# Moving output copies into two-buffer slots, pooling stores to another queue, and the last stage's loads a chunk ahead

## The chip, the core and the metric

The kernel runs on one NeuronCore of a Trainium2 chip. The metric is the device time of one execution in microseconds (us); lower is better. TensorE (PE) does the matrix products, VectorE (DVE), ScalarE (ACT) and GpSimd (POOL) the elementwise work, and SyncE (SP) and ACT issue the DMAs, each from a queue of its own.

## The reference, cut to what matters

One layer of a hybrid encoder: a normed input goes through one projection, whose columns feed three groups. Sizes: 2048 rows, width 1024, 256 memory tokens, groups of width 512, 4 heads of 128.

```python
h = rmsnorm(x, norm_g)
proj = h @ w_in                                   # (2048, 1024) @ (1024, 5128)
qk_raw, v, o, z_a, gates, u, z_b, qc, z_c = split(proj)
y_a = mlstm(conv(qk_raw), v, o, gates) * silu(z_a)     # chunked recurrence, per head rmsnorm
y_b = pool(u) * silu(z_b)                              # window means of 2, 4, 8, 16, minus u, @ pool_w
km, vm = split(rmsnorm(mem, mem_norm_g) @ w_kv)        # 256 memory tokens
y_c = (softmax(qc @ km.T / sqrt(128)) @ vm) * silu(z_c)
x = x + concat([y_a, y_b, y_c]) @ w_out
return rmsnorm(x, final_norm_g)
```

All of it is float32.

## The kernel before, in words

Products are made in three TensorE passes of "fp32r" parts: a tensor is split into a high half (ACT copies it) and a low half (DVE or POOL subtracts), and `mm3` (L152, L155, L156) multiplies high by high, high by low and low by high.

The projection is tiled into **quads**: a block of 2x2 tiles, 2 blocks of 512 rows by two column halves, computed with seven products in place of eight (Winograd's form of Strassen). The quad's combined inputs are the forms `A11`, `A12`, `S1` to `S4`, `A22`, held as tiles `xA`, `xS` (split at L198 on ACT and L199 on DVE); combined weights are the tiles `wf`. Kinds of quad: `run_tok` (the columns v, o, z_a, rows as partitions; results go to the DRAM scratch `d_t`), and channel quads for the convolution, for pooling and for attention. The sequence of 2048 rows is done in two halves s=0 and s=1. Order: one `run_tok` quad with the memory tokens' products laid in between (the first stage), four pairs of convolution and pooling quads, four attention quads, two `run_tok` quads, and for s=1 two `run_tok` quads, four pairs, four attention quads, one `run_tok` quad. Then the output stage runs over 16 chunks of 128 rows.

Work is placed between the products by a list: `later(n, f)` puts `f` n ticks ahead, and each product ends with `tick()`. A scheduler then sets each engine's order from the program and a timeline; each engine runs its list strictly in that order, and a wait stops all behind it. Tiles come from pools: a tag has a number of buffers, and a new tile of a tag waits until the last use of the oldest one is over, its store to DRAM too.

What the change touches:

- `ev` (L141) gives the tiles in which PSUM is copied out. The tags `s1` and `u2` have two buffers each; all other names share the tag `e` with one buffer: `dg` of `bcast` (L163, four diagonals made from row factors at L166, from which the product at L168 broadcasts them to all partitions), `c11` (L420), `c12` (L435), `ga` and `q1`. `run_tok` has for each of its two blocks `bk` the results s1, c11, u2, c12 in turn, and `store` (L397) issues their DMA on ACT's queue (in the trace these tiles are `c`, `s`, `u`, and the DMA is `d_t<-c`).
- `first(n)` (L596) is the list of the first stage: `mem_k`, `mem_v` (keys and values of the memory tokens, 12 products of 128x512 for each `mem_v(q)`), `scale_y` (L183, eight rows `y`, which needs `dg`) and the forms of the next quad.
- `pooling`'s `end` (L844) multiplies by the gate into `zb` and stores its two halves at L847 on SP's queue.
- `load_y(c)` (L956) loads 128 rows of y_b and y_c as `yr` (L959, SP), copies the high half on ACT (`ybh`, L962) and the low half on POOL (`ybl`, L963). It is called for c = 0 during the last `run_tok` quad, for c = 1 ahead of the output stage, and for c + 2 inside chunk c's turn. All `yr` share one slot, `x0`.
- In the attention quads `th` (L782) copies the transposed probabilities for the product with the values.
- The output stage: `out_k(c, i)` (L982) adds twelve steps per chunk, the first eight from y_b and y_c, the last four from y_a. `cell(c)` (L1026) is the recurrence of chunk c: `Ab` gets the mask on POOL (L1029), `Dm` is its exponential on ACT (L1034), multiplied by the scores on DVE (L1048) and used by the products at L1062; the head norm goes `sq` (ACT, L1089), `ss` (DVE, L1090, then POOL's power, L1091), `hh` (DVE, L1093); the transpose of `hh` (L1098) is y_a.

Of the kernel before, what the change touches and what calls it, by code (L numbers as in the profile page):

```python
# [18 lines left out]
P = 128  # L19
# [7 lines left out]
GW = 512  # L27
# [25 lines left out]
def hybrid_block(tc, xT, xn, memT, wch, wuT, wtok, wgt, wkm, wvm, wo, pw, cols, bg, gf, out):  # L53
# [33 lines left out]
    with ExitStack() as outer:  # L87
# [73 lines left out]
            G.tensor_tensor(dst, ms[:, :w], mhalf[:, :w], ALU.pow)  # L161

        def bcast(src_cols, w):  # L163
            dg = ev("dg", shape=(P, 4, P))
            for i in range(w):
                V.tensor_scalar(dg[:, i], ident, src_cols[:, i:i + 1], None, ALU.mult)  # L166
            pb = bank([P, 4, P], "aux")
            tc.keep_in_program_order(T.matmul(pb[:, :w], ones, dg[:, :w], start=True, stop=True))  # L168
            return pb[:, :w].rearrange("p a b -> p (a b)")
# [220 lines left out]
        def run_tok(q, step=None, pinned=False):  # L390
# [9 lines left out]
            for n, (xfm, wfm, acc, opens) in enumerate(q.order):  # L400
# [5 lines left out]
                for bk in range(2):  # L406
                    pp = banks[acc][bk]
                    for r in range(2):
                        sl = slice((2 * bk + r) * P, (2 * bk + r + 1) * P)
                        for k in range(4):  # L410
                            wh, wl = q.forms[wfm][k]
                            xt = xf[xfm][k]
                            mm3(pp[:, r], xt[:, 0, sl], xt[:, 1, sl], wh, wl, opens and k == 0 and r == 0, k == 3,
                                pin=k == 0 and (opens and r == 1 or pinned and r == 0))
                    pf = pp.rearrange("p a b -> p (a b)")
                    if n == 0:
                        s1[bk] = ev("s1")
                        A.activation(s1[bk], pf, AF.Copy)
                    elif n == 1:
                        c11 = ev("c11")  # L420
                        A.activation(c11, pf, func)
                        store(c11, 0, 0, bk)
                    elif n == 2:
                        u2[bk] = ev("u2")
                        V.tensor_tensor(u2[bk], pf, s1[bk], ALU.add)
                    elif n == 3:
                        V.tensor_tensor(s1[bk], pf, u2[bk], ALU.add)
                    elif n == 4:
                        t = s1[bk]
                        V.tensor_tensor(t, pf, t, ALU.add)  # L430
                        if n_:
                            A.activation(t, t, func)
                        store(t, 1, 1, bk)
                    elif n == 5:
                        t = ev("c12")  # L435
                        V.tensor_tensor(t, pf, u2[bk], ALU.add)
                        if n_:
                            A.activation(t, t, func)
                        store(t, 0, 1, bk)
                    else:  # L440
                        t = u2[bk]
                        V.tensor_tensor(t, pf, t, ALU.add)
                        if n_:
                            A.activation(t, t, func)
                        store(t, 1, 0, bk)
                    if bk == 1:
                        used(q, wfm)
                    tick()
# [147 lines left out]
        def first(n):  # L596
# [9 lines left out]
            elif n == 2:  # L606
                scale_y(0, y, 1)
                xs["pre"]()
                Wv.append(mem_w(wvm[0], [P, 2, GW]))
            elif n == 3:  # L610
                mem_k(3, W[3])
                mem_k_out(3)
                Wv.append(mem_w(wvm[1], [P, 2, GW]))
                xs["S2"]()
            elif 4 <= n < 8:
                mem_v(n - 4, Wv[n - 4])
                if n < 6:
                    Wv.append(mem_w(wvm[n - 2], [P, 2, GW]))
            for m, f in ((5, "S1"), (6, "S3"), (8, "S4"), (10, "A22")):
                if n == m:  # L620
                    xs[f]()
        for n in range(12):
# [191 lines left out]
        def pooling(q):  # L814
# [10 lines left out]
            def sums():  # L825
# [18 lines left out]
                def end():  # L844
                    V.tensor_tensor(z, cur[0][:, HL:], z, ALU.mult)
                    for i in range(2):
                        dma(d_y[2 * s + i][:, :, g, :], z[:, i * BW:(i + 1) * BW].rearrange("p (a b) -> p a b", a=4))  # L847
                n = win.bit_length() - 1
                for i in range(n):
                    (add if i == 0 else lambda st: later(i, lambda: add(st)))(1 << i)  # L850
# [87 lines left out]
        def prep_wo(i):  # L938
# [12 lines left out]
            else:  # L951
                g = col[:, C_OG + k:C_OG + k + 1]
                A.activation(woh[k], raw, AF.Copy, scale=g)
                V.scalar_tensor_tensor(wl, raw, g, r32(woh[k]), ALU.mult, ALU.subtract)

        def load_y(c):  # L956
            b, cc = divmod(c, 4)
            yr = xp.tile([P, 8, P], F32, name="yr", tag="x0")
            dma(yr, d_y[b][:, cc])  # L959
            yh = xp.tile([P, 8, P], F32R, name="ybh", tag=f"x{1 + c % 2}")  # L960
            yl = (fp if c % 2 else xp).tile([P, 8, P], F32R, name="ybl", tag="ybl" if c % 2 else "x3")
            A.activation(yh, yr, AF.Copy)  # L962
            G.tensor_tensor(yl, yr, r32(yh), ALU.subtract)  # L963
            return yh, yl

        def last_step(n):
            if n == 2:
                ybs[0] = load_y(0)
            elif n > 2:
                prep_wo(2 * n - 6)  # L970
                prep_wo(2 * n - 5)
# [19 lines left out]
                T.matmul(outs[c][n], l, w[:, n * 512:(n + 1) * 512], start=i == 0 and p_ == 0, stop=i == KO - 1 and p_ == 2)  # L991


        ybs[1] = load_y(1)
        gfb = fp.tile([P, D], F32, name="gfb", tag="gfb")
        dma(gfb, gf.partition_broadcast(P))

# [154 lines left out]
        for c in range(NT):  # L1152
            xr = st([P, D], "xr")
            dma(xr, xn[c * P:(c + 1) * P])
            if c + 1 < NT:
                outs[c + 1] = [bank([P, 512], "mm") for n in range(2)]
                for i in range(8):
# [2 lines left out]
                    out_k(c + 1, i, ybs[c + 1])  # L1160
                    tick()
                    if i == 1 and c + 2 < NT:
                        ybs[c + 2] = load_y(c + 2)
                    if i == 5 and c + 2 < NT:
                        load_chunk(c + 2)
                while c not in yas or (c == NT - 2 and due):
# [60 lines left out]
```

## Time and profile before

| | before |
|---|---|
| device time, median of 3 runs | 1254.31 us (1253.19 to 1255.76) |
| the profiled execution, its own time | 1250.7 us |
| its span, first to last instruction | 1248.9 us |
| PE busy | 1178.2 us, 94% |
| DVE busy | 747.8 us, 60% |
| ACT busy | 481.4 us, 39% |
| POOL busy | 201.8 us, 16% |
| mean granted TensorE clock | 0.976 of full |

The profiled execution is 3.6 us under the median, and 1.8 us of it lie outside the span. The page's first part gives busy times, the second forty slices of the span with the granted clock, the fifth the groups of instructions with the idle time ahead of them. A bracket such as `[2.99 <-ACT th L782]` behind an instruction is the idle time of its engine before it, and what ended that idle time.

### The profile page before, as it was taken

How to read it: one execution, taken by the hardware profiler on the slowest of the kernel's cores; microseconds unless marked ns; L12 is line 12 of the kernel's file. 1: busy time of each engine (PE TensorE's matmuls, PEld its weight loads, DVE VectorE, ACT ScalarE, POOL GpSimd, SP SyncE). 2: the span in 40 equal slices, each digit the busy share in tenths (PEclk: the TensorE clock that was granted, in tenths of full speed). 3: DMA queues.
4: the chain of work that ended last, by engine and by line, in shares of the span. 5: the costliest groups of instructions: out<-in, count | busy, mean ns of one | idle time of the engine just before them, and what ended most of it. 6: DMA issues, size and time to landing. Idle time of an engine off the chain costs nothing. (4 is left out here: it accounts for less than half of the span.)

```text
span 1248.9 us, 17606 instructions
## 1 busy us (share of the span) xinstructions
PE 1178.2 (94%) x6579; PEld 1019.4 (82%) x6579; DVE 747.8 (60%) x1318; ACT 481.4 (39%) x947; POOL 201.8 (16%) x154
## 2 busy tenths in 40 slices
PE   6659999996999899999999999998989999999997
PEld 5649888885888899899778887887978888888886
DVE  5876478976677448842564554554536565656434
ACT  7434454433676434440421224554433222222211
POOL 1321121112001011300000000000035232324120
PEclk9879999999999999999999999998989999999999
DMA  9615877789455698437667775546595545454511
GB/s 355 215 42 203 308 278 281 264 290 317 179 180 191 210 363 301 164 120 246 208 197 227 256 245 207 161 152 219 150 321 163 190 146 179 149 179 145 169 51 68
DMA packets 123925, 258.75 MB, mean 207 GB/s; under 512 B 9792, under 2 KB 65856, under 8 KB 123328
## 3 DMA queue, kind: packets, MB, share of 16 engines
q1 hardware_dynamic: 91680, 230.36, 53.6%
q10 hardware_dynamic: 32160, 27.27, 6.7%
q8 instruction: 52, 0.85, 0.3%
q14 instruction: 33, 0.27, 0.1%
HBM read 158.96 MB, written 98.63 MB: 206 GB/s over the span
## 5 line engine op out<-in xcount | busy, mean ns | idle before, releaser
L307 ACT ACTIVATE wf<-wr 128x512 fp32r<-128x512 f32 x120 | 74.6, 628 | 116.0 <-PE mm L156 66.1
L308 DVE TENSOR_TENSOR wf<-wr,wf 128x512 fp32r<-128x512 f32 x120 | 85.0, 717 | 47.0 <-ACT wf L307 47.0
L152 PE MATMUL mm<-xS,wf 128*128 128x512 f32 x256 | 101.5, 396 | 1.8 <-DVE s L377 1.8
L156 PE MATMUL mm<-xS,wf 128*128 128x512 f32 x256 | 101.3, 396 | 0.0
L155 PE MATMUL mm<-xS,wf 128*128 128x512 f32 x256 | 100.9, 394 | 0.0
L991 PE MATMUL mm<-woh,ybh 128*128 128x512 f32 x256 | 94.8, 405 | 0.0
L991 PE MATMUL mm<-wol,ybh 128*128 128x512 f32 x256 | 92.6, 397 | 0.0
L991 PE MATMUL mm<-woh,ybl 128*128 128x512 f32 x256 | 89.9, 394 | 0.0
L152 PE MATMUL mm<-xA,wf 128*128 128x512 f32 x224 | 89.4, 401 | 0.0
L156 PE MATMUL mm<-xA,wf 128*128 128x512 f32 x224 | 88.5, 395 | 0.0
L155 PE MATMUL mm<-xA,wf 128*128 128x512 f32 x224 | 88.1, 393 | 0.0
L963 POOL TENSOR_TENSOR ybl<-yr,ybh 128x1024 fp32r<-128x1024 f32 x16 | 39.2, 2452 | 196.4 <-ACT ybh L962 156.7
L648 DVE SCALAR_TENSOR_TENSOR cacc<-text,col,cacc 128x1024 f32<-128x1024 f32 x48 | 65.4, 1373 | 8.1 <-ACT cacc L645 7.9
L1093 DVE SCALAR_TENSOR_TENSOR hh<-hh,ss,gz 128x128 f32<-128x128 f32 x64 | 51.4, 862 | 31.2 <-POOL ss L1091 31.2
L156 PE MATMUL pt<-wf,xS 128*128 128x256 f32 x192 | 56.8, 296 | 9.9 <-DVE xS L199 9.9
L152 PE MATMUL pt<-wf,xS 128*128 128x256 f32 x192 | 56.6, 295 | 7.5 <-ACT xS L198 6.2
L291 POOL TENSOR_TENSOR wr<-wr 128x512 f32<-128x512 f32 (+1 forms) x16 | 27.0, 1688 | 218.4 <-DVE wf L308 218.4
L156 PE MATMUL mm<-wf,xA 128*128 128x256 f32 x192 | 55.2, 287 | 4.1 <-DVE xA L199 4.1
L152 PEld LDWEIGHTS mm<-xS,wf 128*128 128x128 f32 x256 | 48.6, 190 | 11.8 <-DVE s L377 2.2
L156 PEld LDWEIGHTS mm<-xS,wf 128*128 128x128 f32 x256 | 48.4, 189 | 11.0
L991 PEld LDWEIGHTS mm<-woh,ybl 128*128 128x128 f32 x256 | 48.1, 188 | 10.7
L155 PEld LDWEIGHTS mm<-xS,wf 128*128 128x128 f32 x256 | 48.5, 190 | 9.9
(303 smaller groups left out, 3260.9 us busy)
## 6 DMA issues: line engine op xcount, KB each, us to landing
wr<-in_wch_dram SPq DMA_DIRECT2D x20, 512.0 KB, 5.4
y<-in_xT_dram SPq DMA_DIRECT2D x32, 256.0 KB, 6.4
wr<-in_wtok_dram SPq DMA_DIRECT2D x16, 512.0 KB, 5.9
d_qk<-cacc ACTq DMA_DIRECT2D x32, 256.0 KB, 4.8
yr<-d_y SPq DMA_DIRECT2D x16, 512.0 KB, 4.5
qk<-d_qk SPq DMA_DIRECT2D x16, 512.0 KB, 3.9
gz<-d_t SPq DMA_DIRECT2D x16, 512.0 KB, 3.7
xr<-in_xn_dram SPq DMA_DIRECT2D x16, 512.0 KB, 3.6
```

Source lines behind the costliest of these rows:

```text
L152: ins = T.matmul(po, ah, bh, start=first, stop=False, skip_group_check=True)
L155: T.matmul(po, ah, bl, start=False, stop=False, skip_group_check=True)
L156: T.matmul(po, al, bh, start=False, stop=last, skip_group_check=True)
L291: G.tensor_tensor(B["B11"], B["B12"], B["B11"], ALU.subtract)
L307: A.activation(t[:, 0], part, AF.Copy)
L308: V.tensor_tensor(t[:, 1], part, r32(t[:, 0]), ALU.subtract)
L648: V.scalar_tensor_tensor(c, t[:, i:i + 2 * BW], w(i), c, ALU.mult, ALU.add)
L963: G.tensor_tensor(yl, yr, r32(yh), ALU.subtract)
L991: T.matmul(outs[c][n], l, w[:, n * 512:(n + 1) * 512], start=i == 0 and p_ == 0, stop=i == KO - 1 and p_ == 2)
L1093: V.scalar_tensor_tensor(hh[:, h], hh[:, h], ss[:, h:h + 1], gz[:, 1, h], ALU.mult, ALU.mult)
```

## The change

Five things. The tiles `dg` and `c11` take the tag `u2`, and `c12` the tag `s1`, in place of the single buffer `e`. In `first`, each `mem_v` is run one step earlier, and the form `S4` too; `S2` is listed with the other forms, behind `mem_v(0)`. The two stores of each pooling quad go through `dma_out`, which is ACT's queue. `load_y` only issues the load, and `split_y` makes the two halves; the load for chunk c+3 follows the split for chunk c+2, and the raw rows alternate between the slot `x0` and a tile of the last stage's own pool. Loads 1 and 2 and the split of 1 stand ahead of the output stage.

```diff
-            dg = ev("dg", shape=(P, 4, P))
+            dg = ev("dg", shape=(P, 4, P), tag="u2")
...
-                        c11 = ev("c11")
+                        c11 = ev("c11", tag="u2")
...
-                        t = ev("c12")
+                        t = ev("c12", tag="s1")
...
-            elif n == 3:
-                mem_k(3, W[3])
-                mem_k_out(3)
-                Wv.append(mem_w(wvm[1], [P, 2, GW]))
-                xs["S2"]()
-            elif 4 <= n < 8:
-                mem_v(n - 4, Wv[n - 4])
-                if n < 6:
-                    Wv.append(mem_w(wvm[n - 2], [P, 2, GW]))
-            for m, f in ((5, "S1"), (6, "S3"), (8, "S4"), (10, "A22")):
+            elif 3 <= n < 7:
+                if n == 3:
+                    mem_k(3, W[3])
+                    mem_k_out(3)
+                    Wv.append(mem_w(wvm[1], [P, 2, GW]))
+                mem_v(n - 3, Wv[n - 3])
+                if n < 5:
+                    Wv.append(mem_w(wvm[n - 1], [P, 2, GW]))
+            for m, f in ((3, "S2"), (5, "S1"), (6, "S3"), (7, "S4"), (10, "A22")):
...
-                        dma(d_y[2 * s + i][:, :, g, :], z[:, i * BW:(i + 1) * BW].rearrange("p (a b) -> p a b", a=4))
+                        dma_out(d_y[2 * s + i][:, :, g, :], z[:, i * BW:(i + 1) * BW].rearrange("p (a b) -> p a b", a=4))
...
+        yraw = {}
+
         def load_y(c):
             b, cc = divmod(c, 4)
-            yr = xp.tile([P, 8, P], F32, name="yr", tag="x0")
-            dma(yr, d_y[b][:, cc])
+            yraw[c] = (fp if c % 2 else xp).tile([P, 8, P], F32, name="yr", tag="yr" if c % 2 else "x0")
+            dma(yraw[c], d_y[b][:, cc])
+
+        def split_y(c):
+            yr = yraw.pop(c)
             yh = xp.tile([P, 8, P], F32R, name="ybh", tag=f"x{1 + c % 2}")
             yl = (fp if c % 2 else xp).tile([P, 8, P], F32R, name="ybl", tag="ybl" if c % 2 else "x3")
             A.activation(yh, yr, AF.Copy)
             G.tensor_tensor(yl, yr, r32(yh), ALU.subtract)
-            return yh, yl
+            ybs[c] = yh, yl
...
-                ybs[0] = load_y(0)
+                load_y(0)
+                split_y(0)
...
-        ybs[1] = load_y(1)
+        load_y(1)
+        load_y(2)
+        split_y(1)
...
-                        ybs[c + 2] = load_y(c + 2)
+                        split_y(c + 2)
+                        if c + 3 < NT:
+                            load_y(c + 3)
```

Three places show what the scheduler makes of it. The lines of the code behind the change are some four to seven higher in number.

PE in the first stage, where the last product of `mem_k` (`mm<-mhl`) ends; `pt<-wf,xS` is the first product of the form S2 and `aux<-mwh,mhl` the first of `mem_v(0)`. Before:

```order
L155 MATMUL mm<-mhl_188,mwh 128x256
L156 MATMUL mm<-mhl_188,mwl 128x256
L152 MATMUL pt<-wf,xS_0_648 128x256
L155 MATMUL pt<-wf,xS_0_648 128x256
L156 MATMUL pt<-wf,xS_0_648 128x256
```

And after:

```order
L155 MATMUL mm<-mhl_188,mwh 128x256
L156 MATMUL mm<-mhl_188,mwl 128x256
L152 MATMUL aux<-mwh,mhl_143 128x512
L155 MATMUL aux<-mwl,mhl_143 128x512
L156 MATMUL aux<-mwh,mhl_143 128x512
```

The twelve products of `mem_v(0)` stand ahead of S2's; before, they stood behind the first 24 of S2.

ACT where the output stage begins; `ybh` are the high halves of chunks 1, 2 and 3, `Dm` those of cells 0 and 1, `sq` that of cell 0. Before:

```order
L438 ACTIVATE c_8052<-c_8052 128x512
L397 DMA d_t_90<-c_8052 128x2x256
L444 ACTIVATE u_7807<-u_7807 128x512
L953 ACTIVATE woh_8136<-woraw,col 128x1024
L397 DMA d_t_91<-u_7807 128x2x256
L444 ACTIVATE u_7845<-u_7845 128x512
L953 ACTIVATE woh_8142<-woraw,col 128x1024
L397 DMA d_t_91<-u_7845 128x2x256
L1034 ACT_TABLE_LOAD
L1034 ACTIVATE Dm<-Ab,tcols 128x128 x8
L962 ACTIVATE ybh<-yr 128x1024
L1089 ACTIVATE sq,ss<-hh 128x128 x4
```

And after:

```order
L444 ACTIVATE u_7807<-u_7807 128x512
L397 DMA d_t_91<-u_7807 128x2x256
L952 ACTIVATE woh_8136<-woraw,col 128x1024
L444 ACTIVATE u_7845<-u_7845 128x512
L952 ACTIVATE woh_8142<-woraw,col 128x1024
L397 DMA d_t_91<-u_7845 128x2x256
L966 ACTIVATE ybh<-yr 128x1024 x2
L1041 ACT_TABLE_LOAD
L1041 ACTIVATE Dm<-Ab,tcols 128x128 x8
L1096 ACTIVATE sq,ss<-hh 128x128 x4
```

The split of chunk 2 has moved from between `Dm` and `sq` to ahead of both, and that of chunk 1 from ahead of `c_8052` to beside it.

POOL at the same place, from the last memset on. Before:

```order
L1029 TENSOR_TENSOR Ab<-Ab,mask 128x512 x2
L1036 TENSOR_TENSOR Eb<-qk,Eb 128x512
L963 TENSOR_TENSOR ybl<-yr,ybh 128x1024
L1091 TENSOR_TENSOR ss<-ss,mhalf 128x4
L1029 TENSOR_TENSOR Ab<-Ab,mask 128x512
L963 TENSOR_TENSOR ybl<-yr,ybh 128x1024
```

And after:

```order
L967 TENSOR_TENSOR ybl<-yr,ybh 128x1024
L1036 TENSOR_TENSOR Ab<-Ab,mask 128x512
L967 TENSOR_TENSOR ybl<-yr,ybh 128x1024
L1036 TENSOR_TENSOR Ab<-Ab,mask 128x512
L1043 TENSOR_TENSOR Eb<-qk,Eb 128x512
L1098 TENSOR_TENSOR ss<-ss,mhalf 128x4
L967 TENSOR_TENSOR ybl<-yr,ybh 128x1024
```

The low half of chunk 2 stood directly ahead of the power of cell 0's norm, and now stands between the two masks.

## Rows read from the trace of the kernel before

**Rows 1.** The page, part 1: busy us, share of the span, instructions

```profile
PE 1178.2 (94%) x6579; PEld 1019.4 (82%) x6579; DVE 747.8 (60%) x1318; ACT 481.4 (39%) x947; POOL 201.8 (16%) x154
```

**Rows 2.** Waits of PE: engine, line, releaser: us in total, times, longest

```profile
PE aux L152 <- ACT th L782: 8.5, 2, 5.5
...
PE aux L168 <- DVE dg L166: 7.3, 1, 7.3
...
PE pt L1062 <- issue: 5.2, 1, 5.2
```

**Rows 3.** Windows: stretch, length, busy us of five engines, granted clock, DMA share, GB/s

```profile
66.40:83.50 17.10, 6.71 (x24) 5.54 (x25) 14.75 (x18) 4.40 (x8) 5.76 (x4) 0.50 0.22 74
...
424.80:428.30 3.50, 3.50 (x19) 3.50 (x18) 0.00 (x0) 0.00 (x0) 0.00 (x0) 0.51 0.46 177
480.80:520.20 39.40, 37.67 (x292) 34.89 (x292) 39.40 (x60) 18.61 (x33) 13.03 (x9) 1.00 0.57 195
867.85:872.00 4.15, 4.14 (x17) 3.70 (x18) 2.56 (x3) 1.48 (x2) 0.00 (x0) 0.50 0.65 218
931.85:936.85 5.00, 5.00 (x22) 4.68 (x23) 2.27 (x11) 1.27 (x2) 2.36 (x1) 0.50 0.80 260
```

**Rows 4.** Timeline, DVE, first stage: start us, us, operation

```profile
50.40 1.21 DVE L519 TENSOR_TENSOR mwl<-mwraw,mwh 128x1024 fp32r<-128x1024 f32 x1
...
51.87 0.86 DVE L166 TENSOR_SCALAR dg<-ident,rt 128x128 f32<-128x128 f32 x4
```

**Rows 5.** Timeline, PE: the first two products of the first value product

```profile
83.53 0.40 PE L152 MATMUL aux<-mwh,mhl 128*128 128x512 f32 x1
83.77 0.39 PE L155 MATMUL aux<-mwl,mhl 128*128 128x512 f32 x1
```

**Rows 6.** Timeline, ACT, at the end of the two attention stages

```profile
421.90 0.60 ACT L421 ACTIVATE c<-mm 128x512 f32<-128x512 f32 x1 [2.06 <-DMA d_t<-c]
...
866.16 0.60 ACT L421 ACTIVATE c<-mm 128x512 f32<-128x512 f32 x1 [3.85 <-DMA d_t<-c]
```

**Rows 7.** Timeline, PE, at the same two places

```profile
423.03 0.49 PE L152 MATMUL aux<-th,vmhl 128*128 128x512 f32 x1 [2.99 <-ACT th L782]
...
867.86 0.79 PE L152 MATMUL aux<-th,vmhl 128*128 128x512 f32 x1 [5.50 <-ACT th L782]
```

**Rows 8.** The tile c: its stores, from issue to landing

```profile
DMA to landing us min/median/max: 2.1/3.9/9.1
```

**Rows 9.** The pooling stores: duration of the issue in ns, first and last

```profile
L847 SPq DMA_DIRECT2D d_y<-zb x16: 524/580/894, 193.0 to 746.6; - x16
```

**Rows 10.** Waits of SP's queue at these stores

```profile
SPq L847 <- DVE zb L845: 7.5, 6, 2.5
```

**Rows 11.** Waits of ACT at the weight copies

```profile
ACT wf L307 <- PE mm L156: 68.3, 34, 9.5
```

**Rows 12.** Timeline, ACT, start of the output stage: the split of chunk 2

```profile
924.28 1.06 ACT L962 ACTIVATE ybh<-yr 128x1024 fp32r<-128x1024 f32 x1 [4.19 <-DMA yr<-d_y]
```

**Rows 13.** Timeline, POOL, same place

```profile
925.47 2.35 POOL L963 TENSOR_TENSOR ybl<-yr,ybh 128x1024 fp32r<-128x1024 f32 x1 [5.47 <-ACT ybh L962]
927.92 1.03 POOL L1091 TENSOR_TENSOR ss<-ss,mhalf 128x4 f32<-128x4 f32 x1
```

**Rows 14.** Timeline, DVE, same place and the end of the last quad

```profile
896.51 1.28 DVE L954 SCALAR_TENSOR_TENSOR wol<-woraw,col,woh 128x1024 fp32r<-128x1024 f32 x1 [1.74 <-ACT woh L953]
...
900.09 3.37 DVE L954 SCALAR_TENSOR_TENSOR wol<-woraw,col,woh 128x1024 fp32r<-128x1024 f32 x1
...
931.07 0.68 DVE L1048 TENSOR_TENSOR Dm<-aux,Dm 128x512 f32<-128x512 f32 x1
```

**Rows 15.** Timeline, PE: the first product of chunk 1, and the gap

```profile
910.51 0.39 PE L991 MATMUL mm<-woh,ybh 128*128 128x512 f32 x1
...
931.86 0.77 PE L1062 MATMUL pt<-vt,Dm 128*128 128x129 f32 x2 [5.15 <-issue]
```

**Rows 16.** The tile yr: its loads, from issue to landing

```profile
DMA to landing us min/median/max: 3.8/4.5/9.0
```

## The prediction

> **What bounds the kernel now.** First the busy times: PE works 94% of the span [rows 1], so what does not shorten PE's own work can win only the remaining 6% and what is lost to a lower clock. Second, therefore, the list of what PE waits for [rows 2]; the reader should look there for waits whose releaser the change touches. Three stand out: 8.5 us on `th`, 7.3 us on `dg`, 5.2 us without a named releaser ahead of the product of `vt` and `Dm`. Third, windows around these places, for the granted clock: after each long gap PE runs for some microseconds at 0.50 to 0.51, which is 1.2 in place of 2.4 GHz [rows 3], so a gap costs more than its own length. Fourth, the timelines of the engine that PE waited for, to see what that engine itself stood at [rows 4, 6, 12 to 14]. The sum below is made against the profiled execution, 1250.7 us; the median of the runs is 3.6 us higher, and I add that at the end. About 0.2%, 2.5 us here, is what a measurement of this kernel can tell from no change.
>
> **The copies c11 and c12.** At the end of each attention stage ACT stands at the second c11: 2.06 us at 421.90 and 3.85 us at 866.16, released by the store of the first one, which holds the only buffer [rows 6]. Right behind it on ACT are the copies `th`, and PE has nothing else: its gaps are 2.99 and 5.50 us [rows 7]. ACT's order there is the same after the change, but c11 takes its second buffer of `u2`, so the first place gains 2.0 us and the second 3.85. What is left of the gaps is about 1.0 and 1.65 us, for the copies and the handover. The clock: PE then worked 3.50 us at 0.51 and 4.15 us at 0.50 [rows 3]; half of that is lost, 1.7 and 2.1 us. That so short a rest leaves the clock up is my choice, with a little taken off the first: 1.5 and 2.05. Together 3.5 and 5.9 us; if the clock falls all the same, 2.0 and 3.85.
>
> What it costs: `u2` now carries `dg`, two c11 and two u2 in turn. The first u2 of a `run_tok` quad takes the first c11's buffer and waits for its store. A product group of a block is 24 passes of 256 columns, 2.8 us at 0.118 us (half of the 0.24 us that a pass of 512 takes [rows 5]), so the use comes two groups, 5.6 us, behind c11. The store lands in 3.9 us as a median, 9.1 at most [rows 8]: usually nothing, at worst 3.5 us of DVE, in front of a PE that has other banks. I take 0 in five quads. In the quad of the second half's start, 457 to 520, the new order puts `dg` and the scaling of `y` ahead of the eviction of u2, and DVE is busy for all of 480.80 to 520.20 [rows 3] while PE works 37.67 of those 39.40 us. So PE can lose up to 2 us at the moved eviction, or gain up to the 1.7 us idle there, and some of the work that DVE starts earlier; 0, from -2 to +4.
>
> **The value products.** From 66.40 to 83.50 PE did the 24 passes of S2's first block in 17.10 us and was busy for 6.71 of them, at half clock, because DVE, busy for 14.75, made the low halves [rows 3]. The twelve passes of `mem_v(0)` came behind it; now they stand ahead. At 0.24 us each from start to start [rows 5] that is 2.8 us at full clock, some 5.2 at half, and both fit in the idle 10.4 us, if the operands are there. So 2.8 us disappear from the later place. DVE's order moves as well: `dg` goes ahead of a `mwl` (1.21 us), a `kmhl` and two weight halves, so it starts about 2.1 us earlier than at 51.87, and what it passed runs while PE makes the broadcast [rows 4]. But the last low half of S2 has one more `mwl` (1.21 us [rows 4]) and one more low half ahead of it (0.68, as a step of 128x512 takes in [rows 14]), 1.9 us: it comes 0.2 us earlier, which I count as nothing. Term: 2.8; bounds 0 (the fill is late, S2 by as much) and 4.9 (the 2.1 us are kept too).
>
> **The pooling stores.** Sixteen issues of 0.58 us [rows 9] leave SP for ACT, two at the end of each of eight quads. They wait in ACT's order for the product into `zb`; SP stood at six of them, 7.5 us in all, 2.5 at most [rows 10]. Behind them on ACT stand weight copies and evictions. ACT has room: at the weight copies alone it waits 68.3 us for PE, in 34 pieces [rows 11], and PE shows no wait of its own there among the large ones. Cost 0; without that cover, 2.5 + 2 x 0.58 = 3.7 us per quad, which is the rival on the slow side.
>
> **The rows of y, a chunk ahead.** In the trace before, the split of chunk 2 stood in the middle of the first cell's norm. ACT waited 4.19 us for the load `yr` and split until 925.34 [rows 12] with `sq` behind it; POOL made `ybl` until 927.82 and only then the power `ss`, until 928.95 [rows 13]; DVE needed that for `hh`, and directly behind `hh` came the product into `Dm` of cell 1 at 931.07 [rows 14]. PE waited for that `Dm`: 5.15 us of gap at 931.86 [rows 15], then 5.00 us at clock 0.50 [rows 3], 2.5 lost. In all 7.65 us. After the change ACT's `sq` stands directly behind `Dm`, POOL makes both low halves before `ss` is due, and DVE takes the `Dm` of cell 1 before the products that need `ss`. So the chain is gone from PE's path. New waits: `yr(1)` now lies in the last stage's own pool, so its load can't be issued before that pool opens, behind two weight loads on SP. The second of these waits for a `wol` that took 3.37 us at 900.09, where one took 1.28 at 896.51 [rows 14]; POOL was making `ybl` just then, which it now does later. I put the issue of `yr(1)` at about 902, its landing 4.5 us later as the median of these loads [rows 16], and `ybh` at about 907.5; PE reaches chunk 1 at 910.51 [rows 15]. With the longest landing, 9.0 us [rows 16], `ybh` ends at about 912, and PE stands 1 to 2 us; the load of `qk` for the first scores goes out behind `yr(1)` too. I take 1.05 us for both and count 6.6 us; bounds 3 (both come late) and 9 (the loads further on, which now stand a chunk ahead, save a little more).
>
> A `wol` beside POOL's `ybl` took 3.37 in place of 1.28 us [rows 14], so 2.1 us more. The two splits that now stand close together on POOL will run beside other DVE work: the last two `wol`, which only the last four steps of chunk 0 want, and the products into `Dm` and `kw` of the first cells. I count nothing for it, since PE has the steps of chunk 1 to do meanwhile. The Trainium skill ("GPSIMD Engine Reference", section "Key points") says that GpSimd shares its SBUF interface with VectorE and contends with VectorE instructions that have two SBUF inputs; the row of 3.37 us agrees. By that rule, with both splits at the cost of that row and PE waiting for it, the sum would be 4.2 us smaller, an estimate of 1239.7 us in place of my 1235.5.
>
> **The sum.** 3.5 + 5.9 + 2.8 + 6.6 = 18.8 us, and 0 for the quad at 457 and for the pooling stores. 1250.7 - 18.8 = 1231.9; on the median of the runs 1235.5 us.
>
> **The rivals.** (a) *New slot waits.* The first u2 waits for the first c11's store in all six `run_tok` quads and c12 for that of s1, and the quad at 457 loses its 2 us. For it: the landing reaches 9.1 us [rows 8]. Against: the median is 3.9. With 1.5 us a quad and the 2 us, 11 of the 18.8 are given back: 1246.5. Chance 0.09.
>
> (b) *The last stage only moves its wait.* `yr(1)` and `qk` land with the longest time, PE stands at chunk 1's start, the clock falls there, and the 6.6 us are gone: 1242. For it: at 931.85 the DMA share is 0.80 [rows 3], so loads queue. Against: by my place of it, 902, `yr(1)` has 8.5 us until 910.51, nearly the longest landing. Chance 0.13.
>
> (c) *ACT stands at the pooling stores*, the slow side. In each pooling quad ACT waits for `zb` and holds up an eviction or a weight copy that PE needs within a few microseconds. Price: up to 3.7 us a quad, 29.6 in eight, so 1235.5 + 29.6 = 1265 at most. It decides from 18.8 / 8 = 2.4 us a quad; below that the kernel stays faster. Half of the price gives 1250. Against it: ACT's long waits for PE [rows 11]. Chance of slower by more than 0.2%: 0.05.
>
> (d) *The change does not do what it says*: c11's copy meets another wait in the same place, since its new buffer was last used by a u2 whose store is equally recent, and the splits land where they were. Only the value product is left: 1251.5. Against: that u2 belongs to a quad that ended long before. Chance 0.04.
>
> **How the numbers follow.** The forecast has 0.69: 1235.5, between 1226 (all upper bounds: 3.7 + 5.95 + 4.9 + 9 + 4 = 27.6 us) and 1247 (all lower bounds: 2.0 + 3.85 + 0 + 3 - 2 = 6.9). Rivals (a) and (b) end inside that. The range 1225 to 1248 leaves out most of (c) and (d) and a little beyond the best case. Faster by over 0.2%, under 1251.8: 0.69 + 0.09 + 0.13 = 0.91, less 0.01 for tails; same: 0.04 from (d) and 0.01; slower: 0.05.
>
> **What would show it.** Right: the waits of ACT's c11 for `d_t<-c` are gone and PE's waits on `th` are near 1 and 1.6 us, with the clock at 1.00 behind them; `aux<-mwh,mhl` lies inside the idle time ahead of S2; no gap of PE over 2 us around 920 to 932 and `sq` directly behind `hh`. Wrong: a wait of DVE or ACT at u2 or c12 for a store; PE waiting at the start of chunk 1 for `ybh`, or at the first scores for `qk`; ACT idle before the pooling stores together with PE gaps between 193 and 747 [rows 9]; a new gap of PE in the quad at 457 to 520.

## The result, and the profile after

The changed kernel takes 1235.95 us as the median of four runs (1233.27 to 1242.65); the kernel before took 1255.03 us in the same set (1253.19 to 1256.92). The ratio is 0.9856, 95% interval 0.9812 to 0.9900. That is 18 us less, with the interval 12.5 to 23.6.

The two profiled executions stand closer together: 1250.7 us before, spans 1248.9 and 1235.6, so 13.3 us. The execution of before was 4.3 us under its median of that set and that of after, 1237.5 us, 1.6 us over its own. What follows is read from the spans, so it explains 13.3 us and not the rest.

The waits of PE (engine, line, releaser: us in total, times, longest) show first what went and what came:

```profile
PE aux L152 <- DMA kmhl<-d_km: 12.1, 2, 6.8
...
PE aux L168 <- DVE dg L166: 5.4, 1, 5.4
PE pt L156 <- DVE xS L199: 5.2, 3, 4.2
PE pt L152 <- ACT xS L198: 4.8, 1, 4.8
...
PE aux L152 <- DMA woraw<-in_wo_dram: 1.9, 1, 1.9
...
PE aux L152 <- ACT th L781: 0.9, 1, 0.9
...
PE aux L1054 <- DMA qk<-d_qk: 0.4, 1, 0.4
```

Two of these were, before:

```profile
PE pt L156 <- DVE xS L199: 9.9, 5, 6.3
...
PE aux L152 <- DMA kmhl<-d_km: 8.1, 1, 8.1
```

Beside [rows 2], the wait put down to `th` fell from 8.5 to 0.9 us. The second gap ahead of that product stands here under another releaser, `woraw`, with 1.9 us, so 2.8 of the 8.5 are left. The wait ahead of the product of `vt` and `Dm` is gone, and about half of the wait for low halves. New is a second wait for `kmhl`, the keys of the attention stage: one before, two now.

Where the 13.3 us lie is seen when the start of the n-th PE instruction is compared in the two traces; how much earlier it starts is called the lead. PE has 6579 instructions in both; the order differs only locally. Worked out from the timelines, us:

| place (time before) | lead of after | change over the stretch | forecast |
|---|---|---|---|
| first stage, to 91 | 7.35 | +7.35 | 2.8 |
| pooling quads and first attention quad, to 323 | 8.47 | +1.1 | 0 |
| second c11, to 433 | 12.38 | +3.9 | 3.5 |
| `run_tok` quads and next weights, to 598 | 7.82 | -4.6 | 0 (-2 to +4) |
| second attention stage, to 781 | 4.06 | -3.8 | 0 |
| second c11, to 875 | 7.86 | +3.8 | 5.9 |
| start of the output stage, to 944 | 13.65 | +5.8 | 6.6 |
| the rest | 13.3 | -0.35 | 0 |

So the medians moved by nearly the forecast 18.8 us, the two traces by 13.3, and the terms do not all agree: the first stage gave 4.5 us more than I had, two stages that I had at nothing took 8.4.

**The copies.** The timeline of ACT at both attention stages (start, us, operation, idle before and releaser):

```profile
410.67 0.60 ACT L421 ACTIVATE c<-mm 128x512 f32<-128x512 f32 x1
...
858.51 0.58 ACT L421 ACTIVATE c<-mm 128x512 f32<-128x512 f32 x1
```

And of PE:

```profile
412.40 0.50 PE L152 MATMUL aux<-th,vmhl 128*128 128x512 f32 x1 [0.89 <-ACT th L781]
...
860.21 0.50 PE L152 MATMUL aux<-th,vmhl 128*128 128x512 f32 x1 [1.91 <-DMA woraw<-in_wo_dram]
```

No c11 waits for its store any more; the gaps of [rows 7] went from 2.99 to 0.89 and from 5.50 to 1.91 us. The windows (stretch, length, busy us by engine, granted clock, DMA share, GB/s) around the two attention stages of the second half:

```profile
744.10:749.80 5.70, 0.43 (x3) 0.04 (x1) 0.69 (x1) 0.00 (x0) 0.00 (x0) 0.84 1.01 422
749.80:754.80 5.00, 5.00 (x15) 4.23 (x16) 0.90 (x3) 2.36 (x6) 0.00 (x0) 0.50 0.20 84
...
859.90:864.00 4.10, 3.56 (x15) 3.25 (x16) 2.57 (x3) 1.90 (x3) 0.00 (x0) 0.59 1.07 384
```

The last line: behind the gap of 1.91 us the clock fell to its lower level all the same, so the second place gave its 3.8 us and not the 2.05 for the clock. The length of the rest alone does not decide this. In the kernel with the last pair of stores back on SP (below) the same product waits 1.91 us as well, and behind that the clock stays up:

```profile
856.20:860.30 4.10, 3.62 (x28) 3.32 (x29) 2.66 (x4) 1.83 (x3) 0.00 (x0) 1.00 1.07 389
```

There this place gives 5.2 us. What makes the difference was not found.

**The new wait.** The first of these windows is the second wait for `kmhl`. The timeline of DVE and ACT there:

```profile
736.99 1.23 DVE L844 TENSOR_TENSOR zb<-usum,zb 128x1024 f32<-128x1024 f32 x1
738.24 1.21 ACTq L846 DMA_DIRECT2D d_y<-zb  x2
739.50 0.66 ACTq L889 DMA_DIRECT2D kmhl<-d_km  x1
740.33 0.45 ACTq L890 DMA_DIRECT2D vmhl<-d_vm  x1
```

The pooling stores stand directly ahead of the loads of the keys and values, on the same queue, and wait for `zb`. In the kernel before, the issue was:

```profile
744.14 0.35 ACTq L890 DMA_DIRECT2D kmhl<-d_km  x1
...
752.26 0.35 PE L152 MATMUL aux<-kmhl,qh 128*128 128x256 f32 x1
```

PE then was 7.8 us later everywhere, so 739.50 now corresponds to 747.3: the load is issued 3.2 us later. And it lands after 10.2 us, with the DMA engines at a share of 1.01; before it landed in 8.0 at most. PE waits 5.27 us and then works 5.00 at clock 0.50.

**The last stage.** The timeline of PE and ACT:

```profile
903.99 1.16 PE L1054 MATMUL aux<-qk 128*128 128x128 f32 x8 [0.44 <-DMA qk<-d_qk]
```

```profile
902.28 1.06 ACT L966 ACTIVATE ybh<-yr 128x1024 fp32r<-128x1024 f32 x1 [2.14 <-PE mm L996]
...
913.79 0.31 ACT L1096 ACTIVATE sq<-hh 128x128 f32<-128x128 f32 x1 [1.62 <-DVE hh L1095]
```

The split of chunk 2 now comes at 902, 11 us ahead of `sq`, and `sq` waits for `hh` alone. The 5.15 us of [rows 15] and the half clock behind them are gone; 0.44 us at the first scores came.

### The profile page after: what moved, and what is told of

Same layout as the page of the kernel before. It is cut to its first block, busy times and chain, and to the rows that moved or that the text cites. A ratio compares the mean times of both kernels' runs of the same rounds, so it can differ in the third digit from the quotient of the medians.

```text
span 1235.6 us, 17625 instructions
## 1 busy us (share of the span) xinstructions
PE 1177.8 (95%) x6579; PEld 1019.9 (83%) x6579; DVE 739.6 (60%) x1318; ACT 481.2 (39%) x947; POOL 213.5 (17%) x154
## 5 line engine op out<-in xcount | busy, mean ns | idle before, releaser
L156 PE MATMUL mm<-wf,xA 128*128 128x256 f32 x192 | 55.8, 291 | 3.7 <-DVE xA L199 3.7
L152 PE MATMUL mm<-wf,xA 128*128 128x256 f32 x192 | 56.7, 295 | 2.0 <-DMA wf<-d_tok1B 2.0
```

Of the source, the lines that this page charges most:

```text
L152: ins = T.matmul(po, ah, bh, start=first, stop=False, skip_group_check=True)
L156: T.matmul(po, al, bh, start=False, stop=last, skip_group_check=True)
```

## The experiments

Twelve kernels, in four sets; each set has its own runs of the kernel before. "Against before" is the ratio of the runs, with its interval, times 1254 us.

| kernel | median us | ratio, 95% | against before, us |
|---|---|---|---|
| the change | 1235.95 | 0.9856 (0.9812 to 0.9900) | -18.1 |
| tags alone | 1239.24 | 0.9888 (0.9863 to 0.9913) | -14.0 |
| tag of dg alone | 1248.12 | 0.9956 (0.9941 to 0.9971) | -5.5 |
| tags of c11, c12 alone | 1243.29 | 0.9901 (0.9886 to 0.9916) | -12.4 |
| value products alone | 1251.29 | 0.9966 (0.9950 to 0.9983) | -4.3 |
| rows of y ahead alone | 1250.81 | 0.9976 (0.9960 to 0.9991) | -3.0 |
| stores on ACT alone | 1257.44 | 1.0027 (1.0008 to 1.0047) | +3.4 |
| the change, stores on SP | 1231.51 | 0.9831 (0.9810 to 0.9852) | -21.2 |
| the same, value products as before | 1232.58 | 0.9839 (0.9818 to 0.9861) | -20.2 |
| the change, last pair on SP | 1227.60 | 0.9803 (0.9779 to 0.9828) | -24.7 |
| the same, S4 on DVE | 1232.48 | 0.9829 (0.9807 to 0.9851) | -21.4 |
| stores on SP, keys early | 1224.04 | 0.9772 (0.9753 to 0.9791) | -28.6 |
| keys early, last pair on SP | 1224.08 | 0.9760 (0.9736 to 0.9785) | -30.1 |

The parts add up to -14.0 - 4.3 - 3.0 + 3.4 = -17.9, and the whole is -18.1. That the two agree so well is in part luck: each part has an interval of some 2 to 3 us to either side, the scheduler sets another order for each kernel, and below are pairs of edits that do not add.

### The pooling stores, back on SP

```diff
-                        dma_out(d_y[2 * s + i][:, :, g, :], ...
+                        dma(d_y[2 * s + i][:, :, g, :], ...
```

> The changed kernel with the pooling stores back on SP's queue. Theory A (the stores on ACT stand right ahead of the load of kmhl before the second attention stage, so it is issued 3 us later and lands later): PE's wait for kmhl at about 744, 5.3 us, and the half clock behind it are gone, so 4 to 8 us under the changed kernel, about 1229 us. Theory B (the load lands late because the DMA engines are full, whichever queue): the wait stays at 4 us or more, and the time is that of the changed kernel, about 1236.

1231.51 us, 4.4 under the change (3.1 by the two ratios, whose intervals overlap, so it is the trace that settles it). PE's waits name what is left of `kmhl`:

```profile
PE aux L152 <- DMA kmhl<-d_km: 9.4, 1, 9.4
```

One wait in place of two: that of the second half, with its half clock, is gone, and theory A holds. The one that remains, at the first attention stage, is longer than the 6.8 us of the change. There the stores on ACT do no harm: two weight copies stand between them and the load, which is issued at 295.8 us in the change and at 296.0 here.

### Only the last pair back on SP

```diff
-                        dma_out(d_y[2 * s + i][:, :, g, :], ...
+                        (dma if s and g == 0 else dma_out)(d_y[2 * s + i][:, :, g, :], ...
```

> The changed kernel with the pooling stores of the last pooling quad of the second half back on SP, the other fourteen left on ACT. Theory A (only the pair ahead of the load of kmhl costs anything): as with all stores on SP, about 1231.5 us, and no wait of PE for kmhl at about 744. Theory B (the stores cost at all eight quads): 1234 to 1236 us.

1227.60 us: 8.4 under the change (6.6 by the two ratios), and 4 under the time that theory A gave. PE's wait for `kmhl` and ACT's issue of the load before the second attention stage:

```profile
PE aux L152 <- DMA kmhl<-d_km: 6.8, 1, 6.8
```

```profile
738.09 0.34 ACTq L889 DMA_DIRECT2D kmhl<-d_km  x1
```

Between 740 and 781 us of the time before, this trace gains 1.9 us of lead where the change lost 3.8. So of the sixteen stores the last two cost some 6 to 8 us, and the other fourteen do no harm that shows; they may even help, since the wait at the first attention stage is 6.8 us with them on ACT and 9.4 in the trace with all on SP. The runs of the two kernels overlap (1225.04 to 1234.62 and 1230.47 to 1234.86), so that gain is likely and not certain.

### The stores alone on the kernel before

```diff
-                        dma(d_y[2 * s + i][:, :, g, :], ...
+                        dma_out(d_y[2 * s + i][:, :, g, :], ...
```

> The kernel before with the pooling stores on ACT alone. Theory A (the last pair stands ahead of the load of kmhl on ACT wherever the rest stands): a wait of PE for kmhl of 3 to 6 us in the second attention stage, where the kernel before has none, and half clock behind it; 2 us gained back at the first attention stage; 1257 to 1260 us. Theory B (it was the other edits that made the load critical; my term of 0 holds by itself): 1253 to 1256 us and no such wait over 1.5 us.

1257.44 us, 3.4 us slower, with an interval that leaves out zero. PE's wait in the second attention stage:

```profile
753.94 0.35 PE L152 MATMUL aux<-kmhl,qh 128*128 128x256 f32 x1 [2.73 <-DMA kmhl<-d_km]
```

The time is that of theory A, the wait a little shorter than it had (2.73 for 3 to 6 us); theory B is out. By the medians this one of the five edits makes the kernel slower by itself. Where the 3.4 us lie is not shown: the profiled execution, 1250.77 us, is the fastest of the twelve and level with the trace of before. It loses 0.5 us in that stage, since before PE lost 2.0 us and the clock there at another wait, and has gained 1.4 at the first attention stage.

### The tags

```diff
-            dg = ev("dg", shape=(P, 4, P))
+            dg = ev("dg", shape=(P, 4, P), tag="u2")
...
-                        c11 = ev("c11")
+                        c11 = ev("c11", tag="u2")
...
-                        t = ev("c12")
+                        t = ev("c12", tag="s1")
```

> The kernel before with the three new tags alone. Theory A (c11's wait was on PE's path at both attention stages): PE's waits on th fall from 2.99 and 5.50 to 1 to 2 us, together 6 to 8 us gained, 2 more from the earlier dg, 2 to 4 lost in the quad at 457 to 520: 1246 to 1250 us. Theory B (slot waits for stores return the gain): within 2 us of the kernel before, 1253 or more.

1239.24 us, more than theory A had: the waits on `th` fell to 2.8 us in all, and the first stage gave 7.4 us in the trace. But 4.4 of these are lost again by 175 us, most of it where PE waits for the first pooling quad's `zb` and the clock falls:

```profile
166.79 0.50 PE L152 MATMUL pt<-xA,wf 128*128 128x512 f32 x1 [1.86 <-DVE zb L379]
```

The trace of the whole change has no such wait. In the quad at 457 to 520 the tags lost 1.7. Then `dg` alone:

> The kernel before with the tag of dg alone. Theory A (most of the first stage's gain is dg's: it is written two weight halves earlier, and DVE's steps behind it meet fewer of POOL's): the product into S2's first block ends 6 to 7.5 us earlier than in the kernel before, total 1246 to 1249 us. Theory B (dg is 2 us earlier and no more, as I had it): 1252.5 us. The waits on th stay at 3 and 5.5 us in both.

1248.12 us, -5.5, as theory A says, and the lead behind S2's first block is 5.9 us, just under its 6 to 7.5; the waits on `th` stayed.

```profile
PE aux L152 <- ACT th L782: 8.6, 2, 5.5
```

And c11 and c12 alone:

> The kernel before with the tags of c11 and c12 alone. Theory A (PE's two waits on th are c11's single buffer): the gaps fall to about 1 and 1.8 us, 7 to 8 us gained with the clock, 1246 to 1247.5 us, and nothing changes in the first stage. Theory B (most of the tags' gain hangs on dg): under 4 us gained, 1250 or more.

1243.29 us, -12.4, more than either theory had. The wait on `th` is 0.9 us (and 1.7 under `woraw`), as expected,

```profile
PE aux L152 <- ACT th L782: 0.9, 1, 0.9
```

but I was wrong that nothing would change in the first stage: there the trace shows 4.8 us of lead. I read it so: with c11 and c12 out of the shared buffer, `dg` has it nearly to itself and waits for no store of theirs, so either edit frees the other. The traces bear it out: with either edit alone `dg` is written from 38.4 or 38.5 us on,

```profile
38.42 2.94 DVE L166 TENSOR_SCALAR dg<-ident,rt 128x128 f32<-128x128 f32 x4 [0.69 <-POOL rt L161]
```

(this is the kernel with `dg`'s tag alone), and with both, where `dg` and c11 share `u2`, at 48.5 as in the change; before, it was 51.87. It fits that the two together (-14.0) give less than their sum (-17.9). For c11 and c12 alone the gain is that of the medians only: the profiled execution, 1249.78 us, is the slowest of the five, and its lead of 5.1 us at 457 is lost by 598.

### The value products

```diff
-            elif 4 <= n < 8:
-                mem_v(n - 4, Wv[n - 4])
+            elif 3 <= n < 7:
+                mem_v(n - 3, Wv[n - 3])
```

> The kernel before with the value products moved up alone. Theory A (they fill idle time of PE ahead of S2, and the half-clock stretch gets shorter too): 4 to 6 us gained, about 1249.5 us. Theory B (my term, the fill alone): 2.8 us, about 1251.7.

1251.29 us, -4.3 (interval -2.1 to -6.3). In its trace the filled place shows: PE's gap ahead of S2 is 2.21 us in place of 6.23.

```profile
68.03 0.39 PE L152 MATMUL pt<-wf,xS 128*128 128x256 f32 x1 [2.21 <-ACT xS L198]
```

But the waits for low halves grew, from 9.9 to 11.9 us, and by 91 us the lead in the trace is 1.0 us, once its start, 1.3 us later than that of before, is taken out.

```profile
PE pt L156 <- DVE xS L199: 11.9, 5, 6.6
```

Taken from the changed kernel instead, with the stores on SP:

> The changed kernel with the stores on SP and without the move of the value products. Theory A (the first stage's gain comes from dg's tag; the value products fill time that comes back as a later S2): within 1.5 us of the same kernel with the move, 1230 to 1233 us. Theory B (they are worth the 2.8 us that I gave them): about 1234.3 us.

1232.58 us with the value products as before, 1231.51 with the move: 1.1 us, with intervals of 2.6 us to either side, and in the traces the two are level behind S2's first block (leads 8.1 and 7.7): the fill gains its 2.8 us, but the last low half starts at 75.35 us with the move and at 72.88 without. Further on they are not level. Without the move PE waits for `zb` as it does with the tags alone,

```profile
165.38 0.50 PE L152 MATMUL pt<-xA,wf 128*128 128x512 f32 x1 [1.90 <-DVE zb L379]
```

and at 200 us its lead is 4.4, with the move 7.1. The wait for `kmhl` then takes the difference: 9.4 us with the move and 8.1 without, and at 323 the leads are 5.3 and 5.1. So beside the tags the move is worth 2.7 us up to the first attention stage, and at the end 0 to 3 us.

### The rows of y ahead

```diff
-        ybs[1] = load_y(1)
+        load_y(1)
+        load_y(2)
+        split_y(1)
...
-                        ybs[c + 2] = load_y(c + 2)
+                        split_y(c + 2)
+                        if c + 3 < NT:
+                            load_y(c + 3)
```

> The kernel before with the rows of y loaded a chunk ahead alone. Theory A (the split of chunk 2 was PE's last wait at 926 to 932): no gap over 2 us there, 5 to 7 us gained, about 1248.5 us. Theory B (the wait moves to chunk 1's start): 0 to 3 us gained, 1251 to 1254, with a wait of PE for ybh or qk around 910.

1250.81 us, -3.0, between the theories. The trace has both sides of it: the gap ahead of the product of `vt` and `Dm` is gone, with its half clock (6 us), and PE waits at the first scores instead:

```profile
915.83 1.16 PE L1055 MATMUL aux<-qk 128*128 128x128 f32 x8 [2.25 <-DMA qk<-d_qk]
```

This is rival (b) in part, 2.25 of its 6.6 us. In the whole change the same wait is 0.44 us.

### Where the runs of one kernel differ

The execution with the last pair on SP that was profiled took 1231.8 us, its median is 1227.6, and its lead behind S2's first block (84 us of the time before) is 2.8 us where that of the change was 7.8 (0.7 of the difference is a later start). The two kernels have the same first hundred rows on PE, DVE, ACT and POOL. POOL's timeline there, in the change:

```profile
66.18 14.62 POOL L208 TENSOR_TENSOR y<-y,y 128x512 f32<-128x512 f32 x4 [4.57 <-DVE y L208]
```

And with the last pair on SP:

```profile
66.88 1.59 POOL L208 TENSOR_TENSOR y<-y,y 128x512 f32<-128x512 f32 x1 [4.57 <-DVE y L208]
70.36 1.58 POOL L208 TENSOR_TENSOR y<-y,y 128x512 f32<-128x512 f32 x1 [1.90 <-DVE y L208]
```

With DVE beside it in the latter:

```profile
67.26 1.75 DVE L199 TENSOR_TENSOR xS<-y,xS 128x512 fp32r<-128x512 f32 x1
68.94 0.68 DVE L208 TENSOR_TENSOR y<-y,y 128x512 f32<-128x512 f32 x1
...
70.74 2.28 DVE L519 TENSOR_TENSOR mwl<-mwraw,mwh 128x1024 fp32r<-128x1024 f32 x1
```

Either POOL gets in between two DVE steps, and the DVE step beside it takes 1.75 in place of 0.68 us (2.28 in place of 1.21 for the larger one), or POOL waits until DVE pauses and DVE loses nothing: of the four steps in 14.62 us the first alone lasts 10.89, the others 1.3 each. All traces of this case with these steps on POOL show the one or the other. The four of kernels without a new tag (before, value products alone, rows alone, stores alone) have DVE stretched, and of the nine with one, only this one has. So the better outcome came in eight of nine profiled executions with a new tag, and in none of four without. To take POOL out:

```diff
-                "S4": lambda: (each(G, b_, b_, a, ALU.subtract), x_split("S4", b_)),
+                "S4": lambda: (each(s4, b_, b_, a, ALU.subtract), x_split("S4", b_)),
...
-        xs = x_steps(y)
+        xs = x_steps(y, V)
```

> The changed kernel with the last pooling pair on SP, and in the first stage the four subtractions for S4 on DVE in place of POOL. Theory A (in the first stage POOL's subtractions stretch DVE's steps of S2 from 0.68 to 1.75 us in some executions and starve in others, which makes the runs of one kernel differ by 4 to 5 us): no step of DVE stretched between 62 and 82, S2's first product group ends about 2.4 us later than in the executions where POOL starves and 2 to 3 earlier than in the others, times within 3 us of each other, near 1229 us. Theory B (the spread of the runs has another source): the runs spread as far as with the last pooling pair on SP alone, 1225 to 1235.

In the trace no DVE step between 62 and 82 us is stretched, and the lead behind S2's first block is 5.0 us, between the 2.8 and the 7.8, as theory A has it. But the runs spread over 9.4 us (1228.41 to 1237.83), as far as without it, as theory B has it, and the median of 1232.48 is no better than the 1227.60 without it. So the two outcomes of POOL are real and worth 4 to 5 us in a trace, and they aren't the main source of the spread; what is, stays open.

### Keys early

The wait for `kmhl` at the first attention stage was the largest that the change left. For the first half, the keys of two heads were put into a pool that is open during the pooling quads, with the stores on SP; in the second half the same load is only split into two:

```diff
+        def load_kv(s):
+            kcm, kvp = pool(f"kv{s}")
+            k01 = kvp.tile([P, 2, 2, NMEM], F32R, name="kmhl", tag="kmhl")
+            dma_out(r32(k01), d_km[:, :, 0:2])
+            kv["km"] = [k01]
+            return kcm
...
+        kcm = load_kv(0)
         mixed_stage(0)
         attention_stage(0)
+        close(kcm)
```

> The changed kernel with the stores on SP, and with the keys of heads 0 and 1 for the first half in a pool of their own, loaded during the first pooling quads. Theory A (PE's 7 to 9 us wait for kmhl at about 300 is the lateness of its issue): the wait is gone, with the half clock behind it 8 to 11 us under the kernel with the stores on SP, 1221 to 1224 us. Theory B (another wait stands behind it, for the query's low half or the softmax): under 4 us gained, 1228 or more.

1224.04 us, 7.5 under the kernel with the stores on SP, near the 8 to 11 of theory A. In the traces 6.6 us of it lie between 300 and 323, at the first attention stage, and the second gains no more than with the load in one piece. The wait that stands behind it is named in PE's list, and is 2.7 us:

```profile
PE aux L152 <- ACT qh L749: 2.9, 2, 2.7
```

Both at once, keys early and only the last pair on SP:

> The changed kernel with the keys of heads 0 and 1 loaded early for the first half, the last pooling pair of the second half on SP and the other stores on ACT. Theory A (the stores on ACT help the first half's load, which the early keys help as well, so their gains overlap): 1221 to 1224 us, about as with the early keys alone. Theory B (the gains add): 1220 or less.

1224.08 us, so the gains overlap, as theory A has it (by the ratios the two kernels are 1.5 us apart, within their intervals). These two are the fastest kernels of the study, 30 us under the kernel before.

## Why the prediction was right, and where it was not

The measured 1235.95 us lie 0.5 us from the forecast 1235.5, and the sign and the size of the change were forecast. That it came so close is luck, as the terms show. Point by point:

**c11** was right as a mechanism and nearly in size: 2.1 and 3.6 us of the two gaps went, for 2.0 and 3.85. The clock was half right: it stayed up behind 0.89 us of rest and fell behind 1.91, and in another kernel it stayed up behind 1.91. The step that failed was "that so short a rest leaves the clock up is my choice".

**The slot waits**, rival (a), did not show as a wait of that kind on PE's list. On DVE they came, as my sign of being wrong had it: c12 now waits for the store of `s1`,

```profile
DVE c L436 <- DMA d_t<-s: 5.5, 3, 3.0
```

where before it waited once, 4.4 us, for that of c11. So rival (a) was right on the wait and wrong on its price. The quad at 457 lost 1.9 us, within the -2 of its bounds, with two new gaps of PE, the other sign that I had named:

```profile
472.41 0.39 PE L152 MATMUL mm<-wf,xA 128*128 128x256 f32 x1 [1.59 <-DMA wf<-d_tok1B]
...
500.66 0.38 PE L152 MATMUL pt<-wf,xS 128*128 128x256 f32 x1 [1.16 <-DVE u L442]
```

Why the weights and `u` come late there was not tested. Another 2.7 us up to 598 have a cause that I did not know (below).

**The first stage** was mis-sized: 2.8 us forecast, 7.35 in the trace, outside its bound of 4.9. The step that failed was the last low half of S2, "it comes 0.2 us earlier, which I count as nothing". It came 5.2 us earlier, before and after:

```profile
80.48 0.68 DVE L199 TENSOR_TENSOR xS<-ye,xS 128x512 fp32r<-128x512 f32 x1
```

```profile
75.26 0.68 DVE L199 TENSOR_TENSOR xS<-ye,xS 128x512 fp32r<-128x512 f32 x1
```

`dg`'s product came 2.8 us earlier (I had 2.1), and the 1.9 us of extra DVE steps were counted right. What I had missed is that in the trace of before four of DVE's steps behind 66 us are stretched by POOL's, by some 1.07 us each, 4.3 in all,

```profile
71.51 1.75 DVE L199 TENSOR_TENSOR xS<-ye,xS 128x512 fp32r<-128x512 f32 x1
```

and that in the trace of after, from 62 us on, none is: 2.8 - 1.9 + 4.3 = 5.2. With the 2.8 us of the fill, which was right, that makes 8.0, near the lead of 7.8 behind S2's first block. The extra DVE steps come with the move, so at this place the move is worth little by itself; what it is worth beside the tags, 2.7 us, shows at the later wait for `zb`.

**The pooling stores** were the wrong term. I had 0, and the move alone costs 3.4 us, the last pair 6 to 8 inside the change. I weighed what ACT has queued behind the stores as weight copies and evictions, and did not look at the DMA issues behind them: the loads of the keys stand right there. In the order of the changed kernel these three rows follow one another, so it could have been seen. Rival (c) named ACT's standing at the stores, with an eviction or a weight copy held up at each of eight quads; what was held up was a load, at one.

**The rows of y** were right: 5.8 for 6.6 us, with 0.44 us of the wait for `qk` that I had named.

So the errors cancelled in part: +4.5 in the first stage, -3.8 and -4.6 in the two stages that I had at 0, -2.1 at the second c11, and the traces are 5.5 us short of the sum. The median came out at the forecast all the same because the profiled executions, 13.3 us apart, are 5 us closer together than the medians, and no trace shows where these 5 us lie. A sum made against one execution carries the offset of that execution, and I had taken it for constant.

## What to carry to other kernels

A DMA that is moved to another engine's queue must be checked against the DMAs already on that queue, not only against the engine's arithmetic: one load of keys behind two stores cost 6 to 8 us. A buffer that is shared by several short-lived tiles couples them in every stage, also where only one of them waits visibly; giving either of two tiles another slot freed the other. An edit that gains time in one stage can lose it at the next wait: see how far a lead lasts before you credit it. Where DVE is saturated and POOL reads SBUF beside it, read the durations of single DVE steps against their usual ones before you fill the idle time of the engine that waits for DVE.

## What the runs showed of the hardware

**POOL and DVE.** An SBUF step of POOL and one of DVE did not share: a DVE step of 0.68 us took 1.75 when POOL's of 1.59 came first, and a step of POOL that takes 1.3 us took 10.89 while DVE's stream had no pause. The Trainium skill ("SBUF — State Buffer", section "SBUF: two separate sides") says that a DVE instruction with two SBUF inputs and a GpSimd instruction that reads SBUF use a shared pair of ports, which whichever starts first holds for its whole instruction while the other blocks. The traces agree, with 1.07 us for the block; that a dense stream of DVE steps can hold POOL off for some 10 us, and that the same order of steps did the one or the other in two executions, is from the traces alone.

**Two queues, the same engines.** The Trainium skill ("DMA: Bandwidth & Descriptors", section "Issuing engines are not separate DMA queues") has it that issuing from another engine saves only the time of the issue. The runs agree for the fourteen other stores, which make no difference clear of noise (1227.60 and 1231.51 us). For the last pair the place of the issue within the queue decided, 3.2 us of it, and the load landed after 10.2 us.

**Two rates of PE at full clock.** Passes of 256 columns ran in one of two rates for tens of microseconds. The same window, before and after:

```profile
525.00:560.00 35.00, 35.00 (x312) 35.00 (x311) 16.86 (x25) 14.81 (x24) 4.80 (x2) 1.00 0.42 141
```

```profile
525.00:560.00 35.00, 35.00 (x299) 35.00 (x298) 11.91 (x18) 10.91 (x18) 1.72 (x1) 1.00 0.43 143
```

312 passes in 35 us are 112 ns each, 299 are 117, both at clock 1.00 and with PE never idle. Over the 600 passes from 522 to 598 that is the 2.7 us that the changed kernel loses there. The kernel with the stores on SP had 311 in that window, that with the keys early and the last pair on SP 300, and the value products alone or the rows of y alone, on the kernel before, 300 as well. So no one edit accounts for it. What sets the rate was not found.
